# Two encoder layers on one core: the experts' weights read in other rows and pieces, and the first loads of layer 1 put in another order

## The chip, the cores and the metric

The kernel runs on one core of one Trainium2 chip. The metric is device microseconds (us) of one execution; the time before is the median of three runs, 2055.79 us (2053.3 to 2058.6). All data are float32, 1024 tokens of 1024 numbers.

## The reference, cut to what matters

Two layers. Each has a mixer (attention in layer 0, a recurrent scan in layer 1, both beside attention to a memory), an output projection, a layer norm, and then a mixture of 16 experts of which each token uses two, followed by a second layer norm:

```python
for i in range(DEPTH):
    ...
    x = layer_norm(ALPHA * x + mixed @ w_out[i], ln_g[i, 0], ln_b[i, 0])
    x = layer_norm(ALPHA * x + moe(x, router_w, router_b, exp_w_gate[i], exp_w_up[i], exp_w_down[i]),
                   ln_g[i, 1], ln_b[i, 1])

def expert_block(args):
    xb, e = args
    hb = jax.nn.silu(xb @ w_gate[e]) * (xb @ w_up[e])   # 1024 -> 512
    return hb @ w_down[e]                               # 512 -> 1024
```

Layer 1 begins with `h = x @ w_in`, a projection of the normed rows.

## The kernel before, in words

**Float32 products.** A float32 product is made of three passes in a faster format. `WeightStream` loads a piece of a weight matrix of 1 MB into `w_raw` (SyncE's DMA queue, line 58), ScalarE casts it to `w_hi` (line 77) and VectorE writes the rest to `w_lo` (line 78); `mm3` (lines 103 to 107) multiplies the three pairs. Four raw buffers and five split buffers go round.

**The experts.** `moe` (line 2127) walks the 16 experts in the order `SEQ`. The first eight numbers take up to 192 tokens each, the others 128; below they are called the large and the small experts, and apart from both ends the two kinds alternate. Of a large expert the first 128 tokens go through `mm3` as block a, and the other 64 as block b, whose high and low parts stand side by side in one tile (`xbc`, `hbc`), so that two matmuls do. Weights are the operand that streams, tokens the one that is loaded (PEld). For an expert, `gate_up` (line 2202) needs four pieces, `down` (line 2266) two; `down` of an expert comes one expert later than its `gate_up`. The list of steps `fill` puts transposes of the next tokens (`xposes`, line 2159) and of the hidden rows (`hposes`, line 2244) between the pieces. After each piece `ahead` (line 2185) loads and splits the next ones, and `flush` then issues the evacuations that wait in `late`. All of this is one program order for each engine: ScalarE, for one, takes casts and evacuations strictly in the order written.

**PSUM.** There are eight banks: four under the tag `dense` (the sums of `gate_up`), two under `rlg` (those of `down`), two under `rtr` (transposes). In `down`, the first output half of block a goes to one `rlg` bank and the second half to the other; block b's two halves take the same two banks again, and so the first matmul of block b (line 2298) needs `ya` (line 2289), the evacuation of block a, to be through. `ya` and `yb` are added to DRAM by an indirect DMA of GpSimd (lines 2291 and 2310), each of which waits for the one before it to land.

**Rows of a piece.** Row k * 128 + p of a weight matrix lies on partition p, so a piece holds four rows of 512 columns for each partition that are not neighbours in DRAM; `down`'s two pieces are the two halves of the columns. The transposes of tokens and of hidden rows take 128 neighbouring columns at a time.

**From layer 0 to layer 1.** After the experts there is a branch (line 2506) on whether any block is left over (none was here), and then `first_chunks` of layer 1 (line 796) builds a list of operations that the small planner `Plan` (line 110) orders by costs written beside them: eight tiles of rows are loaded (line 2407), normed (lines 2439 to 2466, with the scale `ln_g` and the shift `ln_b` of line 243), stored, transposed (line 831) and split (lines 839 and 843); four column blocks of `ml_w_in` are loaded into two raw buffers, cast (line 817) and split (line 812); each block of two row tiles and one column block is then a unit of 24 matmuls. `moe_norm` (line 2398) adds the row loads; it gets the four weight blocks as `extra`. Layer 1's last norm calls it too, with scale and shift already loaded.

Of the kernel before, what the change touches and what calls it, by code (L numbers as in the profile page):

```python
# [7 lines left out]
F = mybir.dt.float32  # L8
# [4 lines left out]
OP = mybir.AluOpType  # L13
# [128 lines left out]
def body(ctx, tc, I, O):  # L142
# [21 lines left out]
    def bank(tag, bufs):  # L164
        return cur["ps"].tile([128, 512], F, tag=tag, name=tag, bufs=bufs)
# [1677 lines left out]
    def out_proj(layer, xsrc, rpool, tl, add_experts):  # L1843
        ws, tiles = tl.ws, tl.tiles
        with sbuf_scope("op", "right") as pool:
# [190 lines left out]
            for q in range(2):  # L2036
                p = bank("rtr", 2)
                for k in range(4):
                    nc.tensor.transpose(p[:, k * 128:(k + 1) * 128], x[:, (4 * q + k) * 128:(4 * q + k + 1) * 128], ident)
# [46 lines left out]
            e.c = tl.qscope.__enter__().tile([128, 8, 128], R, name="xbc0")  # L2086
            p = bank("rtr", 2)
            for k in range(8):
                nc.tensor.transpose(p[:, k * 64:(k + 1) * 64], xb[:, k * 128:(k + 1) * 128], ident[:64, :64])
# [6 lines left out]
    def expert_weights(layer, ws):  # L2096

        wg, wu, wd = I["exp_w_gate"], I["exp_w_up"], I["exp_w_down"]
        regs = {0: 0}

        def ereg(i):
            if i not in regs:
                regs[i] = nc.sync.value_load(rt.order[0:1, i:i + 1], min_val=0, max_val=NE - 1)
            return regs[i]

        def chunk(w, i, k0, nk, c0, ncol):
            def src():
                v = w[layer, bass.ds(ereg(i), 1)] if i else w[layer, 0:1]
                return v.rearrange("o (k p) c -> p (o k) c", p=128)[:, k0:k0 + nk, c0:c0 + ncol]
            return src  # L2110

        def add_gu(i):
            for w in (wg, wu):
                ws.add(chunk(w, i, 0, 4, 0, 512), (4, 512))
                ws.add(chunk(w, i, 4, 4, 0, 512), (4, 512))
# [12 lines left out]
    def moe(layer, rpool, ws, ereg):  # L2128
        seq = SEQ
        with sbuf_scope("mo") as pool:  # L2130
# [28 lines left out]
            def xposes(i):  # L2159

                xa, xb = xg.pop(i)
                h = pool.tile([128, 8, 128], R, name="xah", tag="xah", bufs=2)
                l = pool.tile([128, 8, 128], R, name="xal", tag="xal", bufs=2)
                c = pool.tile([128, 8, 128], R, name="xbc", tag="xbc", bufs=1) if xb is not None else None
                xt[i] = (h, l, c)

                def part(q):
                    p = bank("rtr", 2)
                    for k in range(4):
                        nc.tensor.transpose(p[:, k * 128:(k + 1) * 128], xa[:, (4 * q + k) * 128:(4 * q + k + 1) * 128], ident)  # L2170
                    split_from_psum(h[:, 4 * q:4 * q + 4], l[:, 4 * q:4 * q + 4], p.rearrange("p (k t) -> p k t", k=4))

                def rest():
                    p = bank("rtr", 2)
                    for k in range(8):
                        nc.tensor.transpose(p[:, k * 64:(k + 1) * 64], xb[:, k * 128:(k + 1) * 128], ident[:64, :64])
# [68 lines left out]
            def hposes(i):  # L2245
                th = pool.tile([128, 4, 128], R, name="hah", tag="hah", bufs=2)
                tl = pool.tile([128, 4, 128], R, name="hal", tag="hal", bufs=2)
                tc_ = pool.tile([128, 4, 128], R, name="hbc", tag="hbc", bufs=1) if i < NXP else None
                hT[i] = (th, tl, tc_)

                def full():
                    ha = first_h if i == seq[0] else hs[i][0]
                    p = bank("rtr", 2)
                    for k in range(4):
                        nc.tensor.transpose(p[:, k * 128:(k + 1) * 128], ha[:, k * 128:(k + 1) * 128], ident)
                    split_from_psum(th, tl, p.rearrange("p (k t) -> p k t", k=4))

                def rest():
                    hb = hs[i][1]
                    p = bank("rtr", 2)  # L2260
                    for k in range(4):
                        nc.tensor.transpose(p[:, k * 64:(k + 1) * 64], hb[:, k * 128:(k + 1) * 128], ident[:64, :64])
                    split_from_psum(tc_[:, :, 0:64], tc_[:, :, 64:128], p[:, :256].rearrange("p (k t) -> p k t", k=4))
                return [full] + ([rest] if i < NXP else [])

            def down(i, fill):
                th, tl, tc_ = hT.pop(i)
                la, lb = lists.pop(i)
                hb = tc_
                ya = pool.tile([128, D], F, name="ya", tag="ya", bufs=2)  # L2270
                if hb is not None:
                    yb = pool.tile([64, D], F, name="yb", tag="yb", bufs=1)
                    t3 = pool.tile([64, 512], F, name="t1", tag="t1", bufs=1)
                ws2 = []
                for n in range(2):
                    w = ws.next()
                    ws2.append(w)
                    pa = bank("rlg", 2)
                    for k in range(4):
                        mm3(nc, pa, [th[:, k], tl[:, k]], [w[0][:, k], w[1][:, k]], k == 0, k == 3)  # L2280
                    if n:
                        flush()
                    ahead()
                    flush()
                    if fill:
                        fill.pop(0)()

                    def evac(n=n, pa=pa):
                        nc.scalar.mul(ya[:, n * 512:n * 512 + 512], pa, la[:, 1:2].bitcast(F))  # L2289
                        if n == 1:  # L2290
                            nc.gpsimd.indirect_dma_start(out=accd[layer], out_offset=bass.IndirectOffsetOnAxis(ap=la[:, 0:1], axis=0),  # L2291
                                                         in_=ya, in_offset=None, compute_op=OP.add)
                    late.append(evac)
                for n in range(2 if hb is not None else 0):
                    w = ws2[n]
                    pb = bank("rlg", 2)
                    for k in range(4):
                        nc.tensor.matmul(pb, lhsT=tc_[:, k], rhs=w[0][:, k], start=k == 0, stop=False)
                        nc.tensor.matmul(pb, lhsT=tc_[:, k], rhs=w[1][:, k], start=False, stop=k == 3)
                    flush()  # L2300
                    if fill:
                        fill.pop(0)()

                    def evac(n=n, pb=pb):
                        sl = slice(n * 512, n * 512 + 512)
                        nc.scalar.copy(t3, pb[64:128])
                        nc.vector.tensor_add(t3, pb[0:64], t3)
                        nc.vector.tensor_scalar(yb[:, sl], t3, lb[:, 1:2].bitcast(F), None, op0=OP.mult)
                        if n == 1:
                            nc.gpsimd.indirect_dma_start(out=accd[layer], out_offset=bass.IndirectOffsetOnAxis(ap=lb[:, 0:1], axis=0),  # L2310
                                                         in_=yb, in_offset=None, compute_op=OP.add)
                    late.append(evac)

            PRE = 4
            lists[seq[0]] = early.la, early.lb
# [82 lines left out]
    def moe_norm(layer, plan, pool, dst, nbuf, junk, by_dve, after=None, extra=(), rows=None):  # L2398
# [22 lines left out]
        add_load(1)  # L2421
        add_row("ln_b")
        add_load(2)
        for t in range(3, nbuf):
            if extra:
                extra.pop(0)()
            add_load(t)
        for f in extra:
            f()

        def tile_ops(t):
            if t >= nbuf:
# [150 lines left out]
```

## Time and profile before

| what | value |
|---|---|
| median of three runs | 2055.79 us (2053.3 to 2058.6) |
| the profiled execution's own time | 2056.02 us |
| its span, first to last instruction | 2054.0 us |
| mean granted TensorE clock | 0.961 of full speed |
| busy: PE, DVE, ACT, POOL | 91%, 68%, 53%, 22% |
| weights of the experts | 192 loads of 1 MB each |
| DMA packets | 252978, of which 252836 under 8 KB |

Busy time of PE is that of matmuls, which overlap, so a busy PE is not yet one at its peak; PEld is the load of the operand that stays. Idle time counts where the engine is the one that the end waits for. The span is read in 40 slices of 51 us: the experts of layer 0 are slices 12 to 19 (from about 600 to 1000 us), those of layer 1 slices 31 to 39.

### The profile page before, as it was taken

The page shows a single profiled execution, that of the slowest core. Times are in us where ns is not written, and L with a number is a line of the kernel's source. Part 1 is how long each engine was busy: PE and PEld are TensorE (multiplying, and loading weights), DVE is VectorE, ACT ScalarE, POOL GpSimd, SP SyncE. Part 2 cuts the span into 40 slices and gives each one's busy share as a digit, 9 for nine tenths or more (in the row PEclk, how much of TensorE's full clock was granted, in tenths as well). Part 3 has the DMA queues.
Part 4 walks back from the last instruction along what each step waited for, and adds up shares of the span by engine and source line. Part 5 has one row for each costly group of instructions (what it writes and reads, how often), then busy time and mean ns, then how long its engine had stood idle before and what let it go on. Part 6 is the DMA issues. An engine that isn't in the chain of part 4 may idle for free. (4 is left out here: it accounts for less than half of the span.)

```text
span 2054.0 us, 27927 instructions
## 1 busy us (share of the span) xinstructions
PE 1863.0 (91%) x9860; PEld 1552.1 (76%) x9860; DVE 1401.3 (68%) x2717; ACT 1080.4 (53%) x1772; POOL 457.1 (22%) x386
## 2 busy tenths in 40 slices
PE   7999999998979999999599899998798799999991
PEld 6788888877757877777398778887687587777771
DVE  5466656677767877777576554269878687777775
ACT  4465555662236666666454555444422465666663
POOL 1132222201221222222210000065422121222211
PEclk9999999999979999999799999999899899999996
DMA  5452321135538899999632222111664789999995
GB/s 186 118 134 61 68 56 39 53 121 169 189 130 293 286 297 306 311 309 305 196 128 70 63 82 75 62 32 49 212 207 150 230 267 291 297 309 306 298 286 185
DMA packets 252978, 371.19 MB, mean 181 GB/s; under 512 B 47820, under 2 KB 120868, under 8 KB 252836
## 3 DMA queue, kind: packets, MB, share of 16 engines
q1 hardware_dynamic: 237460, 320.00, 47.5%
q0 software_dynamic: 15376, 49.38, 9.5%
q8 instruction: 79, 1.29, 0.3%
q14 instruction: 63, 0.52, 0.1%
HBM read 300.43 MB, written 65.76 MB: 178 GB/s over the span
## 5 line engine op out<-in xcount | busy, mean ns | idle before, releaser
L78 DVE TENSOR_TENSOR w_lo<-w_raw,w_hi 128x2048 fp32r<-128x2048 f32 (+1 forms) x222 | 470.4, 2126 | 191.9 <-ACT w_hi L77 188.7
L77 ACT CAST w_hi<-w_raw 128x2048 fp32r<-128x2048 f32 (+1 forms) x224 | 396.9, 1780 | 62.9 <-DMA w_raw<-in_exp_w_gate_dram 47.2
L105 PE MATMUL dense<-xT_h,w_hi 128*128 128x512 f32 (+1 forms) x544 | 226.3, 416 | 0.9 <-ACT xT_h L192 0.9
L107 PE MATMUL dense<-xT_h,w_lo 128*128 128x512 f32 (+1 forms) x544 | 208.4, 383 | 1.7 <-DVE w_lo L78 1.7
L106 PE MATMUL dense<-xT_l,w_hi 128*128 128x512 f32 (+1 forms) x544 | 208.1, 383 | 1.0 <-DVE xT_l L193 1.0
L105 PE MATMUL dense<-w_hi,xah 128*128 128x512 f32 x480 | 195.9, 408 | 0.0
L107 PE MATMUL dense<-w_hi,xal 128*128 128x512 f32 x480 | 188.3, 392 | 0.0
L106 PE MATMUL dense<-w_lo,xah 128*128 128x512 f32 x480 | 187.9, 391 | 0.0
L2291 POOL DMA_INDIRECT accd<-ya,la x30 | 80.2, 2675 | 431.1 <-ACT ya L2289 419.6
L105 PE MATMUL dense<-w_hi,yh 128*128 128x512 f32 x288 | 127.6, 443 | 10.7 <-ACT yh L1868 10.6
L106 PE MATMUL dense<-w_lo,yh 128*128 128x512 f32 x288 | 119.9, 416 | 7.6 <-DVE w_lo L93 7.6
L342 ACT ACTIVATE att_p<-att_p,att_st 128x352 f32<-128x352 f32 (+1 forms) x96 | 57.9, 604 | 128.4 <-DVE att_st L340 126.2
L584 POOL TENSOR_TENSOR bias<-bias_raw,masks 128x352 f32<-128x352 f32 (+1 forms) x96 | 85.2, 893 | 163.6 <-DVE att_st L350 145.9
L107 PEld LDWEIGHTS dense<-xT_h,w_lo 128*128 128x128 f32 x544 | 103.6, 191 | 23.2 <-DVE w_lo L78 2.6
L107 PE MATMUL dense<-w_hi,yl 128*128 128x512 f32 x288 | 120.1, 417 | 0.2 <-DVE yl L1801 0.2
L351 DVE TENSOR_SCALAR att_p<-att_p,att_st 128x256 f32<-128x256 f32 (+2 forms) x160 | 112.4, 702 | 5.7
L106 PEld LDWEIGHTS dense<-xT_l,w_hi 128*128 128x128 f32 x544 | 104.6, 192 | 8.3 <-DVE xT_l L193 1.4
L105 PEld LDWEIGHTS dense<-xT_h,w_hi 128*128 128x128 f32 x544 | 104.4, 192 | 8.2 <-ACT xT_h L192 1.0
L105 PE MATMUL rlg<-w_hi,hah 128*128 128x512 f32 x256 | 103.9, 406 | 2.7 <-ACT hah L192 2.7
L107 PEld LDWEIGHTS dense<-w_hi,xal 128*128 128x128 f32 x480 | 90.1, 188 | 20.2
L107 PE MATMUL rlg<-w_hi,hal 128*128 128x512 f32 x256 | 101.4, 396 | 3.5 <-DVE hal L193 3.5
L2215 PE MATMUL dense<-w_hi,xbc 128*128 128x512 f32 x256 | 100.8, 394 | 3.8 <-DVE xbc L193 3.8
(448 smaller groups left out, 4308.9 us busy)
## 6 DMA issues: line engine op xcount, KB each, us to landing
w_raw<-in_exp_w_gate_dram SPq DMA_DIRECT2D x64, 1024.0 KB
w_raw<-in_exp_w_up_dram SPq DMA_DIRECT2D x64, 1024.0 KB
w_raw<-in_exp_w_down_dram SPq DMA_DIRECT2D x64, 1024.0 KB
w_raw<-in_na_w_in_dram SPq DMA_DIRECT2D x20, 512.0 KB
w_raw<-in_w_out_dram SPq DMA_DIRECT2D x8, 1024.0 KB
x1d<-z SPq DMA_DIRECT2D x16, 512.0 KB
accd<-za SPq DMA_DIRECT2D x16, 512.0 KB
z<-accd SPq DMA_DIRECT2D x16, 512.0 KB
```

The costliest lines, as they stand in the source:

```text
L77: self.nc.scalar.copy(h[:, :n], t[:, :n])
L78: (eng or self.nc.vector).tensor_tensor(l[:, :n], t[:, :n], h[:, :n].bitcast(F), op=OP.subtract)
L105: nc.tensor.matmul(out, lhsT=a[0], rhs=b[0], start=first, stop=False)
L106: nc.tensor.matmul(out, lhsT=a[0], rhs=b[1], start=False, stop=False)
L107: nc.tensor.matmul(out, lhsT=a[1], rhs=b[0], start=False, stop=last)
L342: nc.scalar.activation(self.p, self.p, AF.Exp, bias=st[:, 0:1], scale=-1.0, accum_out=st[:, 1:2])
L351: nc.vector.tensor_scalar(self.p, self.p, st[:, 2:3], None, op0=OP.mult)
L584: nc.gpsimd.tensor_tensor(b[:, :nr], rev[:, w0:w0 + nr, u0:u0 + 32], nb.masks[:, half * 3 + kind].rearrange("p (a b) -> p a b", b=32)[:, :nr],
L2215: nc.tensor.matmul(pb, lhsT=c[:, kk], rhs=w[0][:, k], start=kk == 0, stop=False)
L2291: nc.gpsimd.indirect_dma_start(out=accd[layer], out_offset=bass.IndirectOffsetOnAxis(ap=la[:, 0:1], axis=0), in_=ya, in_offset=None, compu ...
```

## The change

Three edits. (1) Row p * 8 + k (for `down` p * 4 + k) of a weight matrix now lies on partition p, so that a piece is one run of 8 KB for each partition; the transposes follow by taking every eighth (every fourth) column. (2) `down`'s two pieces are now halves of the rows, so both `rlg` banks of block a are summed through both pieces and evacuated after them, and block b takes two `dense` banks. (3) In `moe_norm` the weight blocks, the scale and the shift are put ahead of the row loads, which wait in the plan for a mark 9 us later.

```diff
-                    nc.tensor.transpose(..., xa[:, (4 * q + k) * 128:(4 * q + k + 1) * 128], ident)
+                    nc.tensor.transpose(..., every(xa, 8, 4 * q + k), ident)
...
-        def chunk(w, i, k0, nk, c0, ncol):
+        def chunk(w, i, k0, nk):
             def src():
                 v = w[layer, bass.ds(ereg(i), 1)] if i else w[layer, 0:1]
-                return v.rearrange("o (k p) c -> p (o k) c", p=128)[:, k0:k0 + nk, c0:c0 + ncol]
+                return v.rearrange("o (p k) c -> p (o k) c", p=128)[:, k0:k0 + nk]
...
-            ws.add(chunk(wd, i, 0, 4, 0, 512), (4, 512))
-            ws.add(chunk(wd, i, 0, 4, 512, 512), (4, 512))
+            ws.add(chunk(wd, i, 0, 2), (2, 1024))
+            ws.add(chunk(wd, i, 2, 2), (2, 1024))
...
+    def every(x, n, k):
+        return x.rearrange("t (p k) -> t k p", k=n)[:, k]
...
-                for n in range(2):
+                pa = [bank("rlg", 2), bank("rlg", 2)]
+                for c in range(2):
                     w = ws.next()
                     ws2.append(w)
-                    pa = bank("rlg", 2)
-                    for k in range(4):
-                        mm3(nc, pa, [th[:, k], tl[:, k]], [w[0][:, k], w[1][:, k]], k == 0, k == 3)
-                    if n:
-                        flush()
+                    for k in range(2):
+                        for n in range(2):
+                            mm3(nc, pa[n], [th[:, 2 * c + k], tl[:, 2 * c + k]], [x[:, k, n * 512:n * 512 + 512] for x in w],
+                                c + k == 0, c == 1 and k == 1)
                     ahead()
                     flush()
...
+                late.extend([lambda: evac(0), lambda: evac(1)])
+                if hb is None:
+                    return
+                pb = [bank("dense", 4), bank("dense", 4)]
...
-            loads.append(plan.op(ends[t - nbuf] if t >= nbuf else [], ("s", 1.5, lambda: load(t)), lag=2.0))
+            loads.append(plan.op(ends[t - nbuf] if t >= nbuf else [sums_there], ("s", 1.5, lambda: load(t)), lag=2.0))
...
-        add_load(0)
+        for f in extra[:2]:
+            f()
         add_row("ln_g")
-        add_load(1)
         add_row("ln_b")
-        add_load(2)
...
+        for f in extra[2:]:
+            f()
+        sums_there = plan.op([], ("d", 0.0, lambda: None), lag=0.0 if rows else 9.0)
+        for t in range(nbuf):
+            add_load(t)
```

**PE in `down` of a large expert**, the end of block a and the start of block b (a name after `<-` is first the streamed operand, then the loaded one; the number after a name tells buffers apart). Before:

```order
L105 MATMUL rlg_8028<-w_hi_7952,hah_7882 128x512
L106 MATMUL rlg_8028<-w_lo_7953,hah_7882 128x512
L107 MATMUL rlg_8028<-w_hi_7952,hal_7883 128x512
L2298 MATMUL rlg_8048<-w_hi_7926,hbc_7884 128x512
L2299 MATMUL rlg_8048<-w_lo_7927,hbc_7884 128x512
```

and in the change:

```order
L105 MATMUL rlg_7588<-w_hi_7544,hah_7474 128x512
L106 MATMUL rlg_7588<-w_lo_7545,hah_7474 128x512
L107 MATMUL rlg_7588<-w_hi_7544,hal_7475 128x512
L105 MATMUL rlg_7589<-w_hi_7544,hah_7474 128x512
L106 MATMUL rlg_7589<-w_lo_7545,hah_7474 128x512
L107 MATMUL rlg_7589<-w_hi_7544,hal_7475 128x512
L2307 MATMUL dense_7639<-w_hi_7518,hbc_7476 128x512
L2307 MATMUL dense_7639<-w_lo_7519,hbc_7476 128x512
L2307 MATMUL dense_7640<-w_hi_7518,hbc_7476 128x512
```

Block b went from the `rlg` banks to `dense` banks; the number of matmuls is the same.

**SyncE's queue where layer 1 begins**, behind the branch after the experts. Before:

```order
L2407 DMA z_9555<-accd_73 128x1024
L243 DMA ln_g_9557<-in_ln_g_dram 128x1024
L2407 DMA z_9559<-accd_73 128x1024
L243 DMA ln_b_9568<-in_ln_b_dram 128x1024
L2407 DMA z_9572<-accd_73 128x1024
L58 DMA w_raw<-in_ml_w_in_dram 128x8x128
L2407 DMA z_9583<-accd_73 128x1024
L58 DMA w_raw<-in_ml_w_in_dram 128x8x128
```

and in the change:

```order
L58 DMA w_raw<-in_ml_w_in_dram 128x8x128 x2
L243 DMA ln_g_9559<-in_ln_g_dram 128x1024
L243 DMA ln_b_9564<-in_ln_b_dram 128x1024
L58 DMA w_raw<-in_ml_w_in_dram 128x8x128 x2
L2416 DMA z_9575<-accd_73 128x1024
L2416 DMA z_9578<-accd_73 128x1024
L2416 DMA z_9582<-accd_73 128x1024
```

All four weight loads, the scale and the shift now stand ahead of the first row load.

**VectorE there, in the change**, from the statistics of row tile 2 to the last step of its norm (`z_9575`, `z_9578` and `z_9582` are row tiles 0, 1 and 2; ahead of these rows stand the four splits of line 812, the statistics of tile 0 and its scaling):

```order
L2447 BN_STATS ln_st<-z_9582 128x6
L2448 BN_STATS ln_st<-z_9582 128x6
L2449 BN_AGGR ln_mv<-ln_st 128x2
L2450 TENSOR_SCALAR ln_mv<-ln_mv 128x1
L2451 TENSOR_SCALAR ln_mv<-ln_mv 128x1
L2474 SCALAR_TENSOR_TENSOR z_9575<-z_9575,ln_mv,ln_b_9564 128x1024
L2464 TENSOR_SCALAR ln_mv<-ln_mv 128x1
L2471 SCALAR_TENSOR_TENSOR z_9578<-z_9578,ln_mv,ln_g_9559 128x1024
L2471 SCALAR_TENSOR_TENSOR z_9582<-z_9582,ln_mv,ln_g_9559 128x1024
L2474 SCALAR_TENSOR_TENSOR z_9578<-z_9578,ln_mv,ln_b_9564 128x1024
L843 TENSOR_TENSOR xT_l<-xp,xT_h 128x4x128 x2
L2474 SCALAR_TENSOR_TENSOR z_9582<-z_9582,ln_mv,ln_b_9564 128x1024
```

Before, two of the four weight splits stood between the norms of these three tiles; now all four stand ahead of them. On TensorE the transposes of tiles 0, 1 and 2 still stand ahead of the first unit, before and now.

## Rows read from the trace of the kernel before

**Rows 1.** The page's second part: busy tenths of TensorE in 40 slices

```profile
PE   7999999998979999999599899998798799999991
```

**Rows 2.** Busy time by stretches: one quiet stretch of layer 0, two around long waits

```profile
800.00:850.00 50.00, 49.14 (x232) 39.37 (x231) 37.78 (x31) 32.71 (x32) 12.60 (x6) 1.00 0.97 313
...
720.00:730.00 10.00, 8.74 (x32) 7.10 (x33) 8.47 (x9) 6.56 (x8) 2.98 (x1) 0.83 0.99 346
...
1730.00:1740.00 10.00, 6.04 (x18) 4.81 (x19) 6.85 (x6) 6.48 (x8) 3.11 (x1) 0.66 0.94 337
```

**Rows 3.** PE's waits, 600 to 1010 us, then 1620 to 2020 us (total, times, longest)

```profile
PE rlg L2298 <- ACT ya L2289: 6.9, 11, 2.2
...
PE rlg L2298 <- ACT ya L2289: 10.7, 11, 4.4
```

**Rows 4.** ACT's waits from 600 to 1010 us

```profile
ACT w_hi L77 <- DMA w_raw<-in_exp_w_gate_dram: 19.6, 9, 4.4
```

**Rows 5.** Timeline of PE around 626 us (start, duration)

```profile
626.03 0.60 PE L2170 MATMUL rtr<-ident,xa 128*128 128x128 f32 x4
...
626.94 0.39 PE L2298 MATMUL rlg<-w_hi,hbc 128*128 128x512 f32 x1
627.17 0.39 PE L2299 MATMUL rlg<-w_lo,hbc 128*128 128x512 f32 x1
```

**Rows 6.** Timeline of PE, then of PEld, at 630.7 us

```profile
630.71 0.71 PE L2176 MATMUL rtr<-ident,xb 64*128 64x64 f32 x8
...
630.71 0.57 PEld L2176 LDWEIGHTS rtr<-ident,xb 64*128 64x128 f32 x8 [0.36 <-issue]
```

**Rows 7.** Groups of PE by form: the transposes in the experts' loop

```profile
L2170 PE MATMUL rtr<-ident,xa 128*128 128x128 f32 x240 | 35.9, 272 | 0.0
...
L2255 PE MATMUL rtr<-ident,ha 128*128 128x128 f32 x128 | 19.3, 273 | 0.5 <-DVE ha L2200 0.5
...
L2176 PE MATMUL rtr<-ident,xb 64*128 64x64 f32 x112 | 10.0, 229 | 0.0
...
L2262 PE MATMUL rtr<-ident,hb 64*128 64x64 f32 x64 | 7.4, 235 | 0.0
```

**Rows 8.** Groups of PEld by form: a load with neighbouring columns, one with one column repeated

```profile
L2176 PEld LDWEIGHTS rtr<-ident,xb 64*128 64x128 f32 x112 | 8.0, 139 | 5.0 <-issue 4.3 <-DVE xal L193 0.7
...
L1248 PEld LDWEIGHTS pd<-ident,tokq 128*128 128x128 f32 x64 | 7.5, 136 | 5.0 <-DVE ab L1361 4.4 <-ACT sT L1225 0.3
```

**Rows 9.** Timeline of all engines, the end of layer 0's experts

```profile
993.18 1.56 POOL L2291 DMA_INDIRECT accd<-ya,la  x1 [7.27 <-ACT ya L2289]
...
998.46 0.69 ACT L2289 ACTIVATE ya<-rlg,la 128x512 f32<-128x512 f32 x1 [2.01 <-PE rlg L107]
...
1000.98 1.56 POOL L2291 DMA_INDIRECT accd<-ya,la  x1 [6.24 <-issue]
```

**Rows 10.** Timeline of all engines, the start of layer 1

```profile
1007.11 0.35 SPq L2407 DMA_DIRECT2D z<-accd  x1
...
1010.62 0.69 DVE L2439 BATCH_NORM_STATS2 ln_st<-z 128x6 f32<-128x512 f32 x1 [11.28 <-DMA z<-accd]
...
1012.43 1.28 DVE L2463 SCALAR_TENSOR_TENSOR z<-z,ln_mv,ln_g 128x1024 f32<-128x1024 f32 x1
...
1021.53 1.22 DVE L812 TENSOR_TENSOR w_lo<-w_raw,w_hi 128x1024 fp32r<-128x1024 f32 x1
...
1022.78 0.38 SPq L58 DMA_DIRECT2D w_raw<-in_ml_w_in_dram  x1
...
1025.48 1.28 DVE L843 TENSOR_TENSOR xT_l<-xp,xT_h 128x512 fp32r<-128x512 f32 x2
...
1027.46 1.04 ACT L817 CAST qm<-w_raw 128x1024 fp32r<-128x1024 f32 x1 [0.59 <-DMA w_raw<-in_ml_w_in_dram]
...
1031.10 1.94 PE L831 MATMUL xp<-ident,z 128*128 128x128 f32 x8 [7.40 <-DVE z L2466]
```

**Rows 11.** The page, third part: a queue of instruction fetches (packets, MB, share)

```profile
q14 instruction: 63, 0.52, 0.1%
```

More of the change, by code (lines that the diff above doesn't have):

```diff
@@ L2038, in out_proj @@
                 for k in range(4):
-                    nc.tensor.transpose(p[:, k * 128:(k + 1) * 128], x[:, (4 * q + k) * 128:(4 * q + k + 1) * 128], ident)
+                    nc.tensor.transpose(p[:, k * 128:(k + 1) * 128], every(x, 8, 4 * q + k), ident)
                 p = p.rearrange("p (k t) -> p k t", k=4)
@@ L2088, in out_proj @@
             for k in range(8):
-                nc.tensor.transpose(p[:, k * 64:(k + 1) * 64], xb[:, k * 128:(k + 1) * 128], ident[:64, :64])
+                nc.tensor.transpose(p[:, k * 64:(k + 1) * 64], every(xb, 8, k), ident[:64, :64])
             split_from_psum(e.c[:, :, 0:64], e.c[:, :, 64:128], p.rearrange("p (k t) -> p k t", k=8))
@@ L2113, in add_gu @@
             for w in (wg, wu):
-                ws.add(chunk(w, i, 0, 4, 0, 512), (4, 512))
-                ws.add(chunk(w, i, 4, 4, 0, 512), (4, 512))
+                ws.add(chunk(w, i, 0, 4), (4, 512))
+                ws.add(chunk(w, i, 4, 4), (4, 512))
         def add_d(i):
-            ws.add(chunk(wd, i, 0, 4, 0, 512), (4, 512))
-            ws.add(chunk(wd, i, 0, 4, 512, 512), (4, 512))
+            ws.add(chunk(wd, i, 0, 2), (2, 1024))
+            ws.add(chunk(wd, i, 2, 2), (2, 1024))
         for n, i in enumerate(SEQ):
@@ L2169, in part @@
                     for k in range(4):
-                        nc.tensor.transpose(p[:, k * 128:(k + 1) * 128], xa[:, (4 * q + k) * 128:(4 * q + k + 1) * 128], ident)
+                        nc.tensor.transpose(p[:, k * 128:(k + 1) * 128], every(xa, 8, 4 * q + k), ident)
                     split_from_psum(h[:, 4 * q:4 * q + 4], l[:, 4 * q:4 * q + 4], p.rearrange("p (k t) -> p k t", k=4))
@@ L2175, in rest @@
                     for k in range(8):
-                        nc.tensor.transpose(p[:, k * 64:(k + 1) * 64], xb[:, k * 128:(k + 1) * 128], ident[:64, :64])
+                        nc.tensor.transpose(p[:, k * 64:(k + 1) * 64], every(xb, 8, k), ident[:64, :64])
                     split_from_psum(c[:, :, 0:64], c[:, :, 64:128], p.rearrange("p (k t) -> p k t", k=8))
@@ L2254, in full @@
                     for k in range(4):
-                        nc.tensor.transpose(p[:, k * 128:(k + 1) * 128], ha[:, k * 128:(k + 1) * 128], ident)
+                        nc.tensor.transpose(p[:, k * 128:(k + 1) * 128], every(ha, 4, k), ident)
                     split_from_psum(th, tl, p.rearrange("p (k t) -> p k t", k=4))
@@ L2261, in rest @@
                     for k in range(4):
-                        nc.tensor.transpose(p[:, k * 64:(k + 1) * 64], hb[:, k * 128:(k + 1) * 128], ident[:64, :64])
+                        nc.tensor.transpose(p[:, k * 64:(k + 1) * 64], every(hb, 4, k), ident[:64, :64])
                     split_from_psum(tc_[:, :, 0:64], tc_[:, :, 64:128], p[:, :256].rearrange("p (k t) -> p k t", k=4))
@@ L2286, in down, with evac @@
                         fill.pop(0)()
[L2288 to L2299, printed above, removed]
+                def evac(n):
+                    nc.scalar.mul(ya[:, n * 512:n * 512 + 512], pa[n], la[:, 1:2].bitcast(F))
+                    if n == 1:
+                        nc.gpsimd.indirect_dma_start(out=accd[layer], out_offset=bass.IndirectOffsetOnAxis(ap=la[:, 0:1], axis=0),
+                                                     in_=ya, in_offset=None, compute_op=OP.add)
+                late.extend([lambda: evac(0), lambda: evac(1)])
+                if hb is None:
+                    return
+                pb = [bank("dense", 4), bank("dense", 4)]
+                for c in range(2):
+                    w = ws2[c]
+                    for k in range(2):
+                        for n in range(2):
+                            for m in range(2):
+                                nc.tensor.matmul(pb[n], lhsT=tc_[:, 2 * c + k], rhs=w[m][:, k, n * 512:n * 512 + 512],
+                                                 start=c + k + m == 0, stop=c == 1 and k + m == 2)
                     flush()
@@ L2302, in down, with evac_b @@
                         fill.pop(0)()
[L2304 to L2312, printed above, removed]
+                def evac_b(n):
+                    sl = slice(n * 512, n * 512 + 512)
+                    nc.scalar.copy(t3, pb[n][64:128])
+                    nc.vector.tensor_add(t3, pb[n][0:64], t3)
+                    nc.vector.tensor_scalar(yb[:, sl], t3, lb[:, 1:2].bitcast(F), None, op0=OP.mult)
+                    if n == 1:
+                        nc.gpsimd.indirect_dma_start(out=accd[layer], out_offset=bass.IndirectOffsetOnAxis(ap=lb[:, 0:1], axis=0),
+                                                     in_=yb, in_offset=None, compute_op=OP.add)
+                late.extend([lambda: evac_b(0), lambda: evac_b(1)])
             PRE = 4
@@ L2418, in add_row @@
                 rops.append(plan.op([], ("s", 1.5, row), lag=2.0))
-        add_load(0)
+        for f in extra[:2]:
+            f()
         add_row("ln_g")
-        add_load(1)
         add_row("ln_b")
-        add_load(2)
-        for t in range(3, nbuf):
-            if extra:
-                extra.pop(0)()
+        for f in extra[2:]:
+            f()
+        sums_there = plan.op([], ("d", 0.0, lambda: None), lag=0.0 if rows else 9.0)
+        for t in range(nbuf):
             add_load(t)
-        for f in extra:
-            f()
         def tile_ops(t):
```

## The prediction, as it was put on record

> **What bounds the kernel now.** I read the 40 slices first: TensorE is at nine tenths or more in slices 14 to 18 and 32 to 38, the experts' loops, and at one tenth in the last one [rows 1]. The stretch from 800 to 850 us shows what a quiet piece of such a loop looks like: TensorE busy 49.14 of 50 us at full granted clock, VectorE 37.78, ScalarE 32.71, DMA share 0.97 at 313 GB/s [rows 2]. So TensorE is the bound and the DMA engines stand close behind. Matmuls of 512 columns start 0.23 us apart there while one lasts 0.39 [rows 5].
>
> Next come TensorE's waits inside the two loops. One line holds most of them: the first matmul into an `rlg` bank for block b (line 2298) waits for `ya`, the evacuation of block a, 11 times for 6.9 us in layer 0 and 11 times for 10.7 us in layer 1 [rows 3]. The reader should see that the evacuation itself is 0.69 us [rows 9]; the wait comes from ScalarE's order, in which `ya` stands behind casts, and a cast waits for its weights: 19.6 us in nine waits in layer 0 alone [rows 4]. After the longest wait of each layer (2.2 and 4.4 us) the granted clock is 0.83 and 0.66 over ten microseconds, so part of that stretch ran at 1.2 instead of 2.4 GHz [rows 2].
>
> Last, the start of layer 1: rows are asked for at 1007.11, VectorE begins on them at 1010.62, and TensorE finishes the transposes of the third row tile, which stand ahead of its first unit, at 1031.10 + 1.94 = 1033.0 [rows 10]. Until then VectorE works through statistics, norms and two weight splits.
>
> **The change, part by part.**
>
> *Block b in `dense` banks.* In the program's order of the change the first matmul of block b waits for no evacuation: its banks were last used by an earlier expert's sums. The two waits of rows 3 go: 17.6 us. They are counted from the modelled end of the matmul before, 0.39 us after its start, while the next would have started after 0.23; 22 times 0.16 adds 3.6 [rows 3, 5]. Gain **21.2 us**. The lost clock goes with them: 0.17 and 0.34 of 10 us, **5.1 us** [rows 2]. What is late next is a weight piece. Without the stalls the loop asks for its bytes some 3% faster, and the DMA share of 0.97 would reach 1.0; the cover is the next edit. `ya`'s two evacuations now run back to back after both pieces: nothing on TensorE waits for them until the next `down`, one expert later. At the end of a layer it is different: the second-last expert's `ya` is 0.69 us later, its scatter (993.18) too, and the last scatter (1000.98) waits for that one to land [rows 9]. In layer 1 this is on the path to the end: plus **0.7 us**. In layer 0 the next part covers it.
>
> *8 KB pieces.* The bytes and the number of loads stay; the runs get four times longer. At 313 GB/s and a share of 0.97 a 2 KB run costs an engine 0.10 us, four of them 0.41 [rows 2]. No row shows an 8 KB run of weights. I take it as no dearer than four short ones, since nothing is added to the bytes; what it saves is slack of an engine group that does not set the end, so I cost it at nothing by itself.
>
> *Strided transposes.* TensorE streams the identity, so the stride falls on the loads (PEld). Four transposes of 128 rows start (0.60 - 0.272) / 3 = 0.109 us apart, eight of 64 rows (0.71 - 0.229) / 7 = 0.069, and their loads (0.57 - 0.139) / 7 = 0.062 [rows 5 to 8]. The rows show no stationary operand with a step; the nearest is one with a column repeated, 136 ns against 139 [rows 8], which would make it free. The other end is a load of double length, 0.124: that adds 0.015 to each of 368 transposes of 128 rows and 0.055 to each of 176 of 64 rows [rows 7], 15 us. (The 32 in the output projection are left out.) I take **4 us**, near the row that there is, and keep 0 and 15; a gain is excluded, since nothing gets shorter.
>
> *Loads ahead of the rows.* The four weight loads, the scale and the shift move past six row loads on SyncE's queue. The first two weight loads go out as soon as the branch is passed, about when the last `ya` ends, 998.46 + 0.69 = 999.2 [rows 9], into a queue that was idle. A load on a full queue took 4.7 us from issue to cast (1022.78 to 1027.46), a cast 1.04, a split 1.22 [rows 10]. So the first splits end near 1006.2 and 1007.4; the third and fourth load wait for the raw buffers that these free, and **all row loads are queued behind them**. The fourth is issued at 1007.4, lands at 1012.1, is cast and split by 1014.4, and only then does VectorE, in its order, take up the rows. They are asked for at 1007.8, when the last scatter has landed, and are there by 1011.3 (3.5 us, as before). From 1014.4 to the end of row tile 2's norm VectorE has two statistics of 1.81, six steps of 1.28, one of 0.15 and a pair of splits of 1.28: 12.7 us [rows 10]. With the transposes (1.94) TensorE's first unit starts at 1029.0 instead of 1033.0: a gain of **4.0 us**, since TensorE does not stop after that. If the fourth split were not late it would be 7.1; if its transfers crowd the scatter, nothing.
>
> **The sum**, against the profiled execution's own 2056.0 us, which is 0.2 above the median: 2056.0 - 21.2 - 5.1 + 0.7 + 4 - 4.0 = 2030.4. I forecast **2030 us**.
>
> **The rivals.**
>
> *Strided loads at double length.* A load that takes one number out of each short stretch of a row could run at half speed. The load of 64 rows is what its transposes wait for (0.062 of 0.069) [rows 6], so it would show there. For it: the step is 16 or 32 bytes everywhere. Against: no row. Price 15 instead of 4: 2041 us. The Trainium skill, "SBUF — State Buffer", section "Door 1: The DMA port swizzle", says of SBUF lines of 16 bytes that two hits per line are needed for full bandwidth; steps of four or eight float32 columns hit each line once, so by that page this rival would be the outcome. No run here shows such a step.
>
> *The weights take over.* The stretches of the long waits have a DMA share of 0.99 and 0.94 [rows 2], and it is late weights that hold ScalarE [rows 4]. If they come no sooner, TensorE waits for `w_hi` where it waited for `ya`, and the 26.3 us stay: 2056.0 + 0.7 + 4 - 4.0 = 2057 us. Against: the casts run ahead of their use by up to three pieces, and no wait of TensorE in the steady loop names a weight today.
>
> *8 KB runs are slower than four of 2 KB* (the other side). The only packets of that size in the trace are instruction fetches: 63 packets, 0.1% of 16 engines' span, which is 0.001 x 16 x 2054 / 63 = 0.52 us each [rows 11]. If weights paid that, a layer's 100.7 MB, 768 packets for each engine, would take 768 x (0.52 - 0.41) = 85 us more, of which the free twentieth of 400 us covers 20: some 65 us for each layer, about 2185 us. It decides from 0.41 + 20 / 768 = 0.44 us for a packet. Against: an instruction fetch lands elsewhere, and the share is rounded.
>
> **How the numbers follow.** Forecast 0.60, strided loads 0.22, weights take over 0.10, slow 8 KB runs 0.08. The forecast's own bounds are 2023 (no stride cost, 7.1 at layer 1) and 2036 (the clock is not won back). The range takes in the first rival with the same loss of clock, 2041 + 5 = 2046: **2022 to 2046**, which leaves out 0.18. A measurement of this kernel tells 0.3% (6 us) from no change. Forecast and first rival are faster, with a small part of the second: 0.84; the rest of the second is no change: 0.08; slow runs 0.08.
>
> **What would show it.** Right: no wait of line 2307 for `ya`, no half-clock stretch inside the loops, a DMA share below 0.95 there, the transposes of 64 rows still 0.07 us apart, and the first unit of layer 1 near 1019 (1033.0 less 10 us from layer 0's experts and 4 from here), 30 us after the last `ya` instead of 34. Wrong: loads of strided columns longer than 0.14 us in PEld; waits of PE for `w_hi` or `w_lo` in the loop; a DMA share of 1.0 with less than 313 GB/s; or row loads that land later than 12 us after the branch.

## The result: 0.9924 of the time before, in the slow part of the stated range

The median of seven runs is **2040.36 us** (2035.86 to 2047.99), 0.9924 of the kernel before with a 95% interval of [0.9899, 0.995]. The profiled execution took 2037.24 us (span 2035.4): of the 25.6 us that the forecast's sum takes off the profiled 2056.0, 18.8 came; by the medians of the two kernels (2055.43 before, seven runs) it is 15.1. The ratios below leave out one run of the kernel called rows first, which took 2717.69 us at a granted clock of 0.644.

The profile after, first busy time by stretches (the same columns as in [rows 2]: length, then PE, PEld, DVE, ACT, POOL, granted clock, DMA share, GB/s):

```profile
800.00:850.00 50.00, 50.00 (x234) 41.08 (x234) 38.27 (x30) 33.42 (x34) 13.41 (x6) 1.00 0.95 314
720.00:730.00 10.00, 10.00 (x46) 8.23 (x45) 8.61 (x9) 6.80 (x8) 2.97 (x1) 1.00 0.97 342
1730.00:1740.00 10.00, 10.00 (x49) 8.36 (x48) 7.44 (x5) 4.78 (x4) 3.33 (x3) 1.00 1.00 294
...
610.00:620.00 10.00, 9.35 (x36) 7.62 (x37) 7.68 (x5) 8.34 (x7) 0.00 (x0) 0.83 0.97 330
```

TensorE does not pause in the first three stretches, and where the clock was at 0.83 and 0.66 in [rows 2] it is at its full level. The last line shows that a part at 1.2 instead of 2.4 GHz remains at the start of the loop, after a wait of 1.4 us for `xbc`; the loop of layer 1 has the same, and 1.7 us are lost there in each. PE's waits from 600 to 1010 us (total, times, longest) hold none of `down`'s block b any more:

```profile
PE dense L106 <- DVE w_lo L93: 3.8, 1, 3.8
PE dense L2220 <- DVE xbc L193: 1.9, 2, 1.4
PE rlg L105 <- ACT ya L2294: 1.3, 1, 1.3
PE rtr L2260 <- DVE ha L2205: 0.4, 1, 0.4
```

The 6.9 us of [rows 3] are gone, and layer 1's 10.7 too. The first line, in every version, belongs to the output projection ahead of the loop. One new wait for `ya` is left, the last `down`'s for the `down` before it, 1.3 us in each layer. Groups of the experts' loops by form, PE's block b and then PEld's loads for the transposes (count, busy time, mean ns of one):

```profile
L2307 PE MATMUL dense<-w_hi,hbc 128*128 128x512 f32 x128 | 50.5, 395 | 0.0
...
L2175 PEld LDWEIGHTS rtr<-ident,xa 128*128 128x128 f32 x240 | 36.0, 190 | 5.1
...
L2260 PEld LDWEIGHTS rtr<-ident,ha 128*128 128x128 f32 x128 | 20.2, 204 | 4.9 <-DVE ha L2205 2.6
...
L2181 PEld LDWEIGHTS rtr<-ident,xb 64*128 64x128 f32 x112 | 13.4, 200 | 5.0 <-issue 4.3 <-DVE xal L193 0.7
...
L2267 PEld LDWEIGHTS rtr<-ident,hb 64*128 64x128 f32 x64 | 8.9, 211 | 5.7 <-issue 5.7
```

Every strided load is longer: 190 to 211 ns where neighbouring columns took 138 to 140. What that costs is in the timeline of PE and then PEld (start, duration of the whole group):

```profile
626.95 0.60 PE L2175 MATMUL rtr<-ident,xa 128*128 128x128 f32 x4
...
631.62 1.09 PE L2181 MATMUL rtr<-ident,xb 64*128 64x64 f32 x8
...
655.54 0.63 PE L2260 MATMUL rtr<-ident,ha 128*128 128x128 f32 x4
...
658.86 0.69 PE L2267 MATMUL rtr<-ident,hb 64*128 64x64 f32 x4
...
631.62 0.96 PEld L2181 LDWEIGHTS rtr<-ident,xb 64*128 64x128 f32 x8 [0.36 <-DVE xal L193]
...
658.85 0.56 PEld L2267 LDWEIGHTS rtr<-ident,hb 64*128 64x128 f32 x4 [0.36 <-issue]
```

Before, the groups of `ha` and `hb` were:

```profile
654.21 0.60 PE L2255 MATMUL rtr<-ident,ha 128*128 128x128 f32 x4
...
657.51 0.46 PE L2262 MATMUL rtr<-ident,hb 64*128 64x64 f32 x4
```

Four transposes of 128 rows of `xa` still take 0.60 us, as in [rows 5], those of `ha` 0.03 more; eight of 64 rows take 1.09 instead of 0.71 [rows 6], because their loads now follow one another after (0.96 - 0.200) / 7 = 0.109 us and no longer after 0.062. At `hb`'s step of 4 it is (0.56 - 0.211) / 3 = 0.116. Last, the start of layer 1, timeline of SP, POOL, ACT, DVE and PE:

```profile
991.07 2.21 SPq L58 DMA_DIRECT2D w_raw<-in_ml_w_in_dram  x2
993.59 1.93 SPq L243 DMA_DIRECT2D ln_g<-in_ln_g_dram  x1
...
999.48 1.88 SPq L58 DMA_DIRECT2D w_raw<-in_ml_w_in_dram  x2
...
996.25 1.56 POOL L2296 DMA_INDIRECT accd<-ya,la  x1 [5.89 <-issue]
...
1005.64 2.75 SPq L2416 DMA_DIRECT2D z<-accd  x6
...
1007.14 1.04 ACT L817 CAST qm<-w_raw 128x1024 fp32r<-128x1024 f32 x1 [7.46 <-DMA w_raw<-in_ml_w_in_dram]
...
1009.69 1.23 DVE L812 TENSOR_TENSOR qm<-w_raw,qm 128x1024 fp32r<-128x1024 f32 x1 [0.24 <-ACT qm L817]
1010.83 0.68 DVE L2447 BATCH_NORM_STATS2 ln_st<-z 128x6 f32<-128x512 f32 x1
...
1024.70 1.97 PE L831 MATMUL xp<-ident,z 128*128 128x128 f32 x8 [1.68 <-DVE xT_l L843]
```

The rows are asked for 9.4 us after the last scatter's issue (996.25 to 1005.64), where it was 6.1 before (1000.98 to 1007.11) [rows 9, 10], and VectorE takes them up right behind the fourth weight split.

### The profile page after: what moved, and what is told of

It reads as the page before. It is cut to its first block, busy times and chain, and to the rows that moved or that the text cites. A ratio compares the mean times of both kernels' runs of the same rounds, so it can differ in the third digit from the quotient of the medians.

```text
span 2035.4 us, 27934 instructions
## 1 busy us (share of the span) xinstructions
PE 1862.7 (92%) x9860; PEld 1565.3 (77%) x9860; DVE 1399.8 (69%) x2717; ACT 1080.5 (53%) x1772; POOL 462.7 (23%) x386
## 5 line engine op out<-in xcount | busy, mean ns | idle before, releaser
L77 ACT CAST w_hi<-w_raw 128x2048 fp32r<-128x2048 f32 (+1 forms) x224 | 396.4, 1779 | 35.8 <-DMA w_raw<-in_exp_w_gate_dram 16.4
L2296 POOL DMA_INDIRECT accd<-ya,la x30 | 75.2, 2507 | 404.5 <-ACT ya L2294 393.3
L105 PEld LDWEIGHTS dense<-w_hi,xah 128*128 128x128 f32 x480 | 90.7, 189 | 17.3
```

What stands on the lines that cost most here:

```text
L77: self.nc.scalar.copy(h[:, :n], t[:, :n])
L105: nc.tensor.matmul(out, lhsT=a[0], rhs=b[0], start=first, stop=False)
```

## The experiments

Two kinds of numbers are used below for each kernel: its time against the kernel before on the same chip, and three stretches of its profile. A loop is counted from the first matmul that reads `xbc` to the end of the last that reads `hah`; the start of layer 1 from there to the first matmul that reads `xT_h`.

| kernel | median us | ratio, 95% interval | loop 0 | loop 1 | start |
|---|---|---|---|---|---|
| before | 2055 to 2059 | 1 | 388.2 | 395.9 | 34.5 |
| the change | 2040.36 | 0.9924 [0.9899, 0.995] | 382.9 | 383.9 | 32.7 |
| banks only | 2038.02 | 0.9895 [0.9871, 0.992] | 380.4 | 380.2 | 33.5 |
| plain columns | 2033.57 | 0.9869 [0.9846, 0.9891] | 377.4 | 378.2 | 32.0 |
| plain columns, again | 2031.25 | 0.987 [0.9852, 0.9888] | 379.6 | 378.4 | 32.3 |
| step of 2 | 2044.87 | 0.9923 [0.9898, 0.9947] | 383.2 | 385.1 | 32.7 |
| banks undone | 2079.01 | 1.01 [1.0084, 1.0116] | 402.7 | 403.1 | 31.9 |
| rows first | 2041.5 | 0.9917 [0.9891, 0.9943] | 382.3 | 382.2 | 33.9 |
| two ahead | 2027.93 | 0.9858 [0.9834, 0.9883] | 377.2 | 379.0 | 29.6 |
| weights only ahead | 2029.16 | 0.9854 [0.9819, 0.989] | 379.1 | 379.4 | 30.8 |

The two profiles of plain columns show what a loop's time tells: it repeats to some 2 us. The kernel before has a median in each of four series of runs, 2055.43 to 2059.44 us; a ratio is taken within one series.

**Banks only.** The kernel before with one edit:

```diff
-                    pb = bank("rlg", 2)
+                    pb = bank("dense", 4)
```

> The kernel before with one edit: block b's sums go to the dense banks; pieces of 2 KB, plain transposes and the old order of loads stay. Theory: the banks alone bring what the loops gained, and the strided transposes took back 9 to 10 us of it: the waits of the first matmul of block b for ya are gone, no half-clock stretch is left in the loops, and the time is near 2055.4 - 26 = 2029 us, below the changed kernel's 2040. Rival (pieces of 2 KB cannot feed the faster loop): TensorE waits for w_hi or w_lo in its place, the DMA share of the loop is 1.0, and the time lies between 2036 and 2056 us.

The loops took 7.8 and 15.7 us less than before, and the time fell to 0.9895, by some 22 us: less than the 26 expected, and 2038 us is inside the span of times that the rival names. Its mechanism is not there, though one of its signs, a DMA share of 1.0, is. The waits of PE from 1600 to 2010 us start with the two that every version has, and the stretch with the most transfers has PE busy all through:

```profile
PE dense L106 <- DVE w_lo L93: 3.8, 1, 3.8
PE dense L2215 <- DVE xbc L193: 1.9, 2, 1.4
```

```profile
1750.00:1800.00 50.00, 50.00 (x238) 40.71 (x237) 38.37 (x30) 34.52 (x34) 12.66 (x7) 1.00 1.03 327
```

So pieces of 2 KB feed the faster loop even at a DMA share of 1.03: no wait for an expert's weight took the place of the one for `ya`. In the loops the banks alone bring more than the whole change (760.6 us together against 766.8): the rest of it takes back more than it adds. The times agree with that but cannot tell the two apart, since their intervals overlap.

**Plain columns.** The changed kernel with the rows of the weights where they were; loads are still of 4 x 512 and 2 x 1024 numbers:

```diff
-                return v.rearrange("o (p k) c -> p (o k) c", p=128)[:, k0:k0 + nk]
+                return v.rearrange("o (k p) c -> p (o k) c", p=128)[:, k0:k0 + nk]
...
-        return x.rearrange("t (p k) -> t k p", k=n)[:, k]
+        return x[:, k * 128:(k + 1) * 128]
```

> The changed kernel with the rows of the weights laid out as before (row = k * 128 + p) and transposes of 128 neighbouring columns; loads of 4 x 512 and 2 x 1024 numbers stay, so that a run is 2 KB for gate and up and 4 KB for down. Theory (16 + 16 transposes of 64 rows each carry some 0.25 to 0.38 us of longer loads): the transposes of 64 rows start 0.07 us apart again and the time is 9 to 10 us under the changed kernel's, near 2030.5 us. Rival (the long runs were needed to feed the loop): TensorE waits for weights in the loops, and the time is the changed kernel's 2040 us or above.

It came to 0.9869, 11 us under the change (0.9924 - 0.9869 of 2057), where 9 to 10 were expected, with loops 8.8 to 11.2 us shorter together in its two profiles. PEld's loads (by form) and PE's timeline are those of before:

```profile
L2181 PEld LDWEIGHTS rtr<-ident,xb 64*128 64x128 f32 x112 | 8.1, 139 | 5.0 <-issue 4.3 <-DVE xal L193 0.7
```

```profile
630.24 0.71 PE L2181 MATMUL rtr<-ident,xb 64*128 64x64 f32 x8
```

By the durations of the groups the stride costs 14 x (1.09 - 0.71) for `xb`, 16 x (0.69 - 0.46) for `hb` and 32 x 0.03 for `ha` (0.63 instead of 0.60), nothing for `xa`: 5.3 + 3.7 + 1.0 = 10.0 us, within what the loops show. Beside banks only, plain columns differ by the longer runs, `down`'s order and the loads at layer 1: its loops are 2.6 to 5.0 us shorter together. That is hardly more than two profiles of one kernel differ by, and no run parts the three.

**Step of 2.** The changed kernel with row j * 256 + 2 * p + i on partition p, so that a transpose takes every second column (the view of the raw tile follows):

```diff
-                return v.rearrange("o (p k) c -> p (o k) c", p=128)[:, k0:k0 + nk]
+                return v.rearrange("o (j p i) c -> p (o j) (i c)", p=128, i=2)[:, k0 // 2:(k0 + nk) // 2]
...
-        return x.rearrange("t (p k) -> t k p", k=n)[:, k]
+        return x.rearrange("t (j p i) -> t j i p", p=128, i=2)[:, k // 2, k % 2]
```

> The changed kernel with a step of 2 float32 instead of 4 or 8 (row = j * 256 + 2 * p + i; runs of 4 KB for gate and up, 8 KB for down). Theory (a load pays by the number of 16-byte lines it touches per number it takes; a step of 2 takes two of each line): the loads of 64 rows take 0.062 us each as for neighbouring columns, the transposes of 64 rows start 0.07 us apart, and the time is that of plain columns, near 2030.5 us. Rival (any step doubles the load): 0.116 us apart, and the changed kernel's 2040 us.

The theory falls, the rival holds: a step of 2 is as dear as one of 4. PEld by form, then PE's timeline:

```profile
L2175 PEld LDWEIGHTS rtr<-ident,xa 128*128 128x128 f32 x240 | 38.1, 203 | 4.7
L2260 PEld LDWEIGHTS rtr<-ident,ha 128*128 128x128 f32 x128 | 20.2, 203 | 4.0 <-DVE ha L2205 1.6
...
L2181 PEld LDWEIGHTS rtr<-ident,xb 64*128 64x128 f32 x112 | 14.4, 212 | 5.0 <-issue 4.3 <-DVE xal L193 0.7
L2267 PEld LDWEIGHTS rtr<-ident,hb 64*128 64x128 f32 x64 | 8.8, 209 | 5.7 <-issue 5.7
```

```profile
634.74 1.17 PE L2181 MATMUL rtr<-ident,xb 64*128 64x64 f32 x8
...
634.74 1.03 PEld L2181 LDWEIGHTS rtr<-ident,xb 64*128 64x128 f32 x8 [0.36 <-DVE xal L193]
```

The loads of `ha` and `hb` take 203 and 209 ns, at a step of 4 it was 204 and 211. Eight transposes of 64 rows take 1.17 us, more than the 1.09 at a step of 8, and their loads follow one another after (1.03 - 0.212) / 7 = 0.117 us. Among steps of 2, 4 and 8, what counts is that the columns are not neighbours, and hardly how far apart they lie.

**Banks undone.** Plain columns with block b behind block a's evacuation again, which has to be issued first for that:

```diff
-                pb = [bank("dense", 4), bank("dense", 4)]
+                flush()
+                pb = [bank("rlg", 2), bank("rlg", 2)]
```

> The kernel with plain columns, with the banks undone: block b's sums go to the rlg banks again, behind block a's evacuation; pieces and loads as in that kernel. Theory (the banks are what the loops gained): the first matmul of block b waits for ya in each of the 16 downs that have a block b, 0.8 us or more each, longer where ScalarE stands behind a cast, half-clock stretches may come back, and the loops together take 15 to 26 us more: 2049 to 2060 us on the scale where plain columns take 2033.6. Rival (the longer runs and earlier weights would have cured the waits by themselves): less than 6 us more, and no wait for ya of over 0.5 us.

The sign was right and the size was not: the loops take 48 us more than in the profile on the same chip (402.7 + 403.1 against 379.6 + 378.4), twice to three times what was expected, though 14 of the 16 `down`s wait and not all. PE's waits from 600 to 1010 and from 1600 to 2010 us:

```profile
PE rlg L2308 <- ACT ya L2294: 15.4, 7, 4.0
...
PE rlg L2308 <- ACT ya L2294: 17.9, 7, 4.6
```

A wait is now 2.4 us where it was 0.8 in [rows 3], since the new order of `down` ends both halves of block a at once, with the casts in ScalarE's order ahead of both evacuations. 33.3 us of waits, 14 x 0.16 of modelled ends as in the forecast, and 2 x 6.8 us of lost clock (by stretches of 10 us, 8.5 us in each loop against 1.7 with the banks) come to 49. The new order of `down` needs the `dense` banks: without them plain columns are slower than the kernel before.

**Rows first.** The changed kernel with the old order of the loads at layer 1's start:

```diff
-            loads.append(plan.op(ends[t - nbuf] if t >= nbuf else [sums_there], ("s", 1.5, lambda: load(t)), lag=2.0))
+            loads.append(plan.op(ends[t - nbuf] if t >= nbuf else [], ("s", 1.5, lambda: load(t)), lag=2.0))
...
-        for f in extra[:2]:
-            f()
+        add_load(0)
         add_row("ln_g")
+        add_load(1)
         add_row("ln_b")
-        for f in extra[2:]:
-            f()
-        sums_there = ...
-        for t in range(nbuf):
+        add_load(2)
+        for t in range(3, nbuf):
+            if extra:
+                extra.pop(0)()
             add_load(t)
```

> The changed kernel with the old order of loads at the start of layer 1: rows of the first tiles, scale and shift first, weights behind them. Theory (the loads ahead of the rows gain 1.6 us there, by the stage's time in the two traces): 2042 us, 1 to 2 us over the changed kernel, and the last scatter of layer 0 as quick as before (4.5 us or less from ya to its issue). Rival (the loads that crowd the last scatter cost more than the early splits bring): at or under 2040 us, with the third tile's transposes no more than 32.2 us after the last ya.

The start is 1.2 us longer than in the change, close to the 1.6 of the theory, but the time cannot tell the two apart (0.9917 and 0.9924). Its timeline of POOL and SP shows the last scatter as quick as before:

```profile
993.57 1.56 POOL L2296 DMA_INDIRECT accd<-ya,la  x1 [5.30 <-DVE xm L880]
...
999.87 0.34 SPq L2416 DMA_DIRECT2D z<-accd  x1
```

Rows 6.3 us after the scatter's issue here, 9.4 in the change: something that goes out ahead of them slows the scatter.

**Two ahead.** Plain columns, with the third and fourth weight load tied to the third row load:

```diff
-        for f in extra[2:]:
-            f()
...
         for t in range(nbuf):
             add_load(t)
+            if 2 <= t < len(extra):
+                extra[t](dep=[loads[2]])
```

> The kernel with plain columns (the second experiment) with one edit at the start of layer 1: only two of the four loads of weights, scale and shift go ahead of the rows; the third and fourth load wait until the third row tile is asked for. Theory (the third and fourth load, issued at 992.7 us between the last scatter and the rows, crowd that scatter): the row loads go out about 6.3 us after the last scatter's issue, as in the kernel with the old order, and not 9.1; TensorE's first unit comes 3 to 6 us sooner after the last expert's matmul than the 32.0 us there, and the time falls by as much, to some 2029 us on the scale where plain columns take 2033.6. Rival (the scatter is slow for another reason, such as the two first loads and the rows of scale and shift): the row loads still go out 9 us after it, and the time stays.

The start became 2.4 us shorter than in the first profile of plain columns, just under the 3 to 6 expected, but for another reason. Its timeline of POOL and SP, then the first stretches in which the scatter is under way:

```profile
991.47 1.56 POOL L2296 DMA_INDIRECT accd<-ya,la  x1 [5.41 <-issue]
...
1000.78 2.24 SPq L2416 DMA_DIRECT2D z<-accd  x5
```

```profile
991.00:993.00 2.00, 0.00 (x0) 0.00 (x0) 0.00 (x0) 0.39 (x1) 1.53 (x1) 0.93 1.16 354
993.00:995.00 2.00, 0.00 (x0) 0.00 (x0) 1.23 (x1) 1.55 (x2) 0.02 (x1) 0.50 1.03 380
```

The rows still go out 9.3 us after the scatter, and the DMA engines are full in the 4 us after its issue. So the third and fourth load were not what crowded it. What was won: their splits no longer stand ahead of the rows on VectorE, and the planner put two row tiles instead of three ahead of the first unit. It has the lowest median of all, and by the intervals it is faster than the kernel before and the change; its ratio of 0.9858 cannot be told from that of plain columns or of the next kernel.

**Weights only ahead.** The same kernel with scale and shift behind the first rows:

```diff
-        add_row("ln_g")
-        add_row("ln_b")
...
             add_load(t)
+            if t < 2:
+                add_row(("ln_g", "ln_b")[t], loads[t:])
```

> The kernel with two loads ahead, with scale and shift behind the first rows again: only two loads of weights, 1 MB, go out before the last scatter, instead of 2.1 MB. Theory (the last scatter is slow because the DMA engines are still moving the bytes that were asked for ahead of it; two loads ahead left it at 9.3 us from issue to the rows, so the later loads were not the cause): with half the bytes ahead, the rows go out 6.3 to 7.5 us after the last scatter's issue. The time itself hardly moves, since the rows' norms then wait for scale and shift, and a third tile stands ahead of the first unit: 2028 us give or take 4. Rival (it is not the bytes ahead but something else that the new order changes): the rows still go out 9 us after the scatter.

Timeline of POOL and SP, then of DVE:

```profile
992.87 1.56 POOL L2296 DMA_INDIRECT accd<-ya,la  x1 [5.37 <-DVE xm L881]
...
999.38 1.29 SPq L2416 DMA_DIRECT2D z<-accd  x3
...
1006.68 0.69 DVE L2447 BATCH_NORM_STATS2 ln_st<-z 128x6 f32<-128x512 f32 x1 [1.87 <-DMA z<-accd]
...
1008.37 1.27 DVE L2471 SCALAR_TENSOR_TENSOR z<-z,ln_mv,ln_g 128x1024 f32<-128x1024 f32 x1
```

6.5 us: with scale and shift (512 KB each) gone from ahead of the scatter, it is as quick as before. Having them there as well as the two weight loads is what crowded it; whether any other 1 MB would do the same is not shown. The time stays, as expected, but no wait for scale or shift shows in VectorE's trace: its statistics of the first tile begin 2.8 us sooner after the last `ya` than with two ahead (1003.03 less 991.73, against 1004.26 less 990.20), and then the planner's order puts the statistics of a second tile, which wait 1.87 us for their rows, ahead of the first scaling. That begins 0.8 us later (16.6 us after the last `ya` against 15.8), and three row tiles instead of two stand ahead of the first unit.

## Why the prediction was right, and by how much its terms were off

The sign, the range and the mechanism of the main term held. The forecast's own bounds, 2023 to 2036 us, did not: 2040 is inside the range only because the range takes in the first rival. That the rival's 2041 was met so closely is in part luck. It priced the stride at 15 us where 10 were measured, and the banks and the loads gave 5 us less than the sum has (26.3 against 23.5, 4.0 against 1.8).

In the profiled executions the change gave 18.6 us of span: loops 784.1 - 766.8 = 17.3, the start of layer 1 1.8, the rest little. The terms as measured, 23.5 - 10.0 + 1.8, make 15.3 of it; the other 3.3 are of the size by which the loops of plain columns beat those of banks only (2.6 to 5.0), and what in them brings it is not shown. The 0.7 us for the last scatter cannot be seen: from the end of layer 1's loop to the end of the span it is 40.6 us before and 40.8 in the change.

*Block b in `dense` banks* was forecast at 21.2 + 5.1 = 26.3 us. Banks only measured 23.5 in the loops and about 22 in the time. Layer 1's part was as said (15.7 against 10.7 + 1.8 + 3.4 = 15.9), layer 0's 2.6 us less. Of these, 1.7 are clock: the forecast has layer 0's lost 1.7 us [rows 2] come back, but banks only, like the change, still loses as much in each loop to a part at 1.2 GHz, in layer 0 at another place than before:

```profile
620.00:630.00 10.00, 10.00 (x44) 7.79 (x43) 6.84 (x7) 6.60 (x8) 2.03 (x2) 0.83 0.97 352
```

That TensorE would stop nowhere else in the steady loop was right, and with it the rival *the weights take over* is out: even runs of 2 KB kept up. With the new order of `down`, `ya` has one wait of 1.3 us in each layer which the forecast did not count.

*Strided transposes* are **the step that failed**: "I take 4 us, near the row that there is". They cost 10. The row it leaned on, a load with one column repeated [rows 8], is no stand-in for a step. The rival *strided loads at double length* priced the part of the 64 rows rightly (176 x 0.055 = 9.7 against 5.3 + 3.7 = 9.0) and that of the 128 rows too high (5.5 against 1.0), because there the load of 0.109 us hides behind a stream that also takes 0.109 [rows 5, 7]; at the step of 4 the load takes 0.116, and 128 x 0.007 is the 0.9 or so of `ha`. So this rival was right in its mechanism and, by the runs, two thirds of its price. The Trainium skill's rule behind it ("SBUF — State Buffer", section "Door 1: The DMA port swizzle", 16-byte lines) foretold the outcome of the change and not that of the step of 2, which hits each line twice and is as slow; there the measurement decides.

*Loads ahead of the rows*: 4.0 forecast, 1.8 by the profiles. The order was as described, down to the fourth split that VectorE finishes ahead of the rows: 15.2 us after the last `ya` by the forecast, 16.4 measured (1010.92 - 994.52). That the two lie so close is in part luck: the first load went out at 991.07, 3.4 us before the last `ya` had ended and not at its end, and the third took 7.7 us from issue to cast (999.48 to 1007.14) where 4.7 were taken. Behind the fourth split, VectorE was through with the third tile's norm after 11.9 us (forecast 12.7), but the transposes ended only after 15.8 us instead of 14.6, since TensorE waited 1.68 us for the split of the tile before. The clause "if its transfers crowd the scatter, nothing" named a risk that was real (9.4 us for 6.1), and the loads of scale and shift made it so. The late rows themselves cost nothing, for they were hidden behind the fourth split: VectorE took up the first of them without a wait. Whether the same crowding held up the third load is not shown.

*8 KB pieces*, costed at nothing, are within a few microseconds of it: the rival of slow 8 KB runs is out, since DMA's share in the loop fell from 0.97 to 0.95 at the same GB/s [rows 2]. The change's loops less the 10.0 us of the stride are 756.8, those of plain columns, with runs of 2 and 4 KB, 755.6 and 758.0.

*The signs.* No wait of line 2307 for `ya` and none for an expert's weight: as said. The other signs of being right failed: the DMA share in the quiet stretch is 0.95 and not below it, half-clock parts remain in the loops, the transposes of 64 rows start (1.09 - 0.277) / 7 = 0.116 us apart, and the first unit starts at 1026.32, 31.8 us after the last `ya`. Two signs of being wrong came: strided loads of 0.19 to 0.21 us, and rows that are asked for only 14.6 us after the branch (991.07 to 1005.64). A share of 1.00 at 294 GB/s stands in one stretch of 10 us, where TensorE does not pause.

*Two readings of rows* were off and leave the sum as it is. In [rows 1] slice 32 is at seven tenths; the run of nines is 33 to 39. And before the change three weight splits, not two, stood ahead of the third tile's norm; this is the third:

```profile
1028.54 1.22 DVE L812 TENSOR_TENSOR qm<-w_raw,qm 128x1024 fp32r<-128x1024 f32 x1 [0.52 <-ACT qm L817]
```

## What to carry to other kernels

A bank that is taken again at once ties TensorE to the slowest thing in the evacuating engine's order; where another tag has banks to spare, that is the edit to make first, and alone. A layout that makes a DMA's runs longer at the price of a strided stationary operand pays on TensorE where the stream is too short to cover the load: look for transposes of few rows before choosing it, and ask whether the transfers were the bound at all. Loads that are put ahead of a dependent chain should be counted against the last transfer of the stage before.

## What the runs showed of the hardware

- In transposes of 64 rows, a load of 128 float32 columns follows another after 0.062 us when the columns are neighbours, and after 0.117, 0.116 and 0.109 us at steps of 2, 4 and 8. The Trainium skill, "TensorE: Matmul & The Clock Gate", section "LDWEIGHTS (loading the stationary operand)", puts a load at its number of columns divided by 1.2 ns: 107 ns for 128. Strided loads here are near that (109 to 117), the transposes' loads of neighbouring columns 1.7 to 1.9 times as fast. Why is not shown, but the short load is not what neighbouring columns always get: the loads of the matmuls, of 128 neighbouring columns too, last 0.19 us and follow one another after 0.11, like strided ones (kernel before, PEld):

```profile
626.36 0.19 PEld L2298 LDWEIGHTS rlg<-w_hi,hbc 128*128 128x128 f32 x1
626.47 0.19 PEld L2299 LDWEIGHTS rlg<-w_lo,hbc 128*128 128x128 f32 x1
```

- An indirect add of 512 KB takes 6.1 to 6.3 us from its issue to the row loads that wait for it, and 8.7 to 9.4 us when 2 MB were asked for in the 4 to 6 us before that (six profiles). With 1 MB ahead it took 6.5 (one profile).
